# Gate and up projections of a SwiGLU block as one unit, with one of four k groups by Strassen's seven products

## The chip, the cores and the metric

The kernel runs on one core of a Trainium2 chip. The metric is device microseconds of one execution, the median of several runs: 2181.53 us before the change (three runs, 2178.58 to 2182.27). The profile shows one further execution of 2179.35 us; its span, from the first to the last instruction, is 2177.2 us. Engines are called as the profile calls them: PE (TensorE; PEld its weight loads), DVE (VectorE), ACT (ScalarE), POOL (GpSimd), SP (SyncE, which here only issues DMAs).

## The reference

One decoder layer on 256 tokens with 2048 channels, all in float32:

```python
def swiglu(x, w_gate, w_up, w_down):
    return (jax.nn.silu(x @ w_gate) * (x @ w_up)) @ w_down

h = h + 0.5 * swiglu(rms_norm(h, ffn1_norm[l]), ffn1_w_gate[l], ffn1_w_up[l], ffn1_w_down[l])
...
h = h + jnp.concatenate([ret, swa.astype(h.dtype)], axis=-1) @ w_out[l]
h = h + memory_cross_attention(rms_norm(h, xa_norm[l]), rms_norm(mem, mem_norm[l]),
                               xa_wq[l], xa_wkv[l], xa_wo[l])
h = h + 0.5 * swiglu(rms_norm(h, ffn2_norm[l]), ffn2_w_gate[l], ffn2_w_up[l], ffn2_w_down[l])
return rms_norm(h, final_norm)
```

Between the two feed-forward networks (FFN 1 and FFN 2) stand retention, sliding-window attention and cross-attention to a memory; the change doesn't touch them. w_gate and w_up are 2048 x 5632, w_down is 5632 x 2048.

## The kernel before

**Precision.** Float32 products are made of a high and a low half. `halves` (L71, L76) writes the high half on ACT (a copy that rounds to float32r) and the low half on DVE (value minus high half). `three` (L450 to L454) then makes three matmuls for each product: high by high, high by low, low by high. Weights are split right before use, a piece of 128 x 1024 at a time, into the tiles wh and wl (four buffers each); the normalized activations are split once into the tiles blk.

**Tiling.** The activations are the stationary operand (128 channels by 128 tokens), the weights the moving one (512 columns). A `Unit` computes 512 columns for all 256 tokens: its accumulator acc has two PSUM banks, one for each token half, and there are two such accumulators. A *step* takes one piece of weights, two k tiles of 128, and makes 2 token halves x 2 k tiles x 3 = 12 matmuls. The 2048 input channels are 16 k tiles, in four *k groups* of four (`norm.blocks`, tiles blk), so a gate or up unit has 8 steps. An FFN has 11 column blocks b of 512. For each, a gate unit and then an up unit run. `gate_done` applies silu with the row scale on ACT (L489), `up_done` multiplies on DVE (L496). `cross` then turns the block, so that its columns lie on partitions: two DVE transposes (L430) into a tile t4k, a DMA from SP into a DRAM tile box (L434), four DMAs from POOL back into t4k (L439), and `halves_of` splits the result into a blk tile `acts[b]` (an ACT copy and a DVE subtraction for each token half).

**Order.** `run_stream` (L230) walks over all steps of all units. It splits the weights of a step three steps ahead (`prepare`, LOOKAHEAD) and loads them eight steps ahead (`fetch`, AHEAD; three buffers wf of two pieces, one DMA of 1 MB from SP each). A clock counts steps; `later` queues work for a number of steps ahead: the box's write after 1, its read after 2, `halves_of` after 6 (TURN). Each engine runs its own instructions in one fixed order, set when the program is built: a scheduler may move an instruction past others of its engine, and then the order stands.

**Down projection.** In both FFNs column blocks 0 to 5 form a first group and 6 to 10 a second. After a group's gate and up units come four down units (one for each 512 output columns, nb), whose steps run over the group's blocks in order, two steps for each. In FFN 2, `turn_h` sends the residual through `cross` too, 19, 35, 51 and 67 steps after the last block of the residual is there.

## Time and profile before

| | |
|---|---|
| time, median of 3 runs (range) | 2181.53 us (2178.58 to 2182.27) |
| the profiled execution | 2179.35 us, span 2177.2 us |
| DVE, ACT, POOL busy | 1285.3, 1025.8, 149.5 us |
| HBM read, written | 443.08 MB, 33.55 MB |
| mean granted TensorE clock | 0.999 |

A row of the groups gives line, engine and operation, output and inputs by the program's names, shape and count; then busy time and the mean of one in ns; then the engine's idle time ahead of these instructions and what ended it. A row of the timeline gives start, duration, engine, line, operation, and in brackets the idle time before it and its releaser. A row of the windows gives the stretch and its length, then the busy time and count of PE, PEld, DVE, ACT and POOL, the granted clock, the DMA engines' share and GB/s. The records of matmuls overlap (389 ns each, one every 227 ns), so their pace is read from their starts.

### The profile page before, as it was taken

The numbers are of one execution on the slowest core, as the hardware profiler recorded it, in microseconds if no ns is written. First come the engines' busy times: TensorE is split into PE (matmuls) and PEld (weight loads), VectorE is DVE, ScalarE is ACT, GpSimd is POOL, SyncE is SP. The second block draws the span as 40 slices with busy tenths as digits, with TensorE's granted clock in tenths as the row PEclk, the third lists the DMA queues.
The fourth block names the chain that finished last, engine by engine and source line by source line (L and its number), as shares of the span: only waits on it lengthen the run. The fifth ranks groups of instructions, "written<-read, shape, count | busy, mean of one in ns | idle before, by whom it ended". The sixth has DMA issues, their size and how long they took to land.

```text
span 2177.2 us, 25112 instructions
## 1 busy us (share of the span) xinstructions
PE 2164.3 (99%) x9772; PEld 1793.3 (82%) x9772; DVE 1285.3 (59%) x1509; ACT 1025.8 (47%) x1260; POOL 149.5 (7%) x257
## 2 busy tenths in 40 slices
PE   9999999999999999999999999999999999999998
PEld 7888888888888888888888888888888888888886
DVE  6555555555556678787675655575555544555554
ACT  6444444444445554546454544454444433444443
POOL 0000000000001010100111100000101000000000
PEclk9999999999999999999999999999999999999999
DMA  7666677666667666556867765676767655666664
GB/s 271 232 221 213 213 232 222 222 213 221 224 216 252 216 216 222 193 186 238 265 231 244 225 216 174 204 243 216 247 222 256 216 193 193 213 213 213 225 210 145
DMA packets 137528, 478.27 MB, mean 220 GB/s; under 512 B 11713, under 2 KB 12481, under 8 KB 137281
## 3 DMA queue, kind: packets, MB, share of 16 engines
q1 hardware_dynamic: 125600, 445.03, 59.5%
q0 software_dynamic: 11520, 31.47, 6.2%
q8 instruction: 76, 1.25, 0.2%
q14 instruction: 44, 0.35, 0.0%
q10 hardware_dynamic: 288, 0.18, 0.0%
HBM read 443.08 MB, written 33.55 MB: 219 GB/s over the span
## 4 chain that ended last, share of the span: by engine, by line
PE 95%; DMA 2%; DVE 1%; issue 1%; ACT 0%; POOL 0%; SPq 0%; ACTq 0%; POOLq 0%; DVEq 0%
PE acc L452 31%; PE acc L453 31%; PE acc L454 31%; DMA wf<-in_ffn_w_up 1%; DMA t4k<-box 1%; DVE wl L76 1%; DMA box<-t4k 0%; PE tmp L454 0%; PE tmp L453 0%; PE tmp L452 0%; ACT wh L71 0%; PE tmp L656 0%; PE tmp L637 0%; PE tmp L603 0%; PE tmp L730 0%
## 5 line engine op out<-in xcount | busy, mean ns | idle before, releaser
L76 DVE TENSOR_TENSOR wl<-wf,wh 128x1024 fp32r<-128x1024 f32 (+1 forms) x776 | 941.4, 1217 | 782.8 <-ACT wh L71 779.0
L71 ACT ACTIVATE wh<-wf 128x1024 fp32r<-128x1024 f32 (+1 forms) x776 | 815.7, 1055 | 982.4 <-PE acc L454 940.2
L452 PE MATMUL acc<-wh,blk 128*128 128x512 f32 (+1 forms) x3104 | 1207.1, 389 | 1.7 <-ACT wh L71 1.1
L453 PE MATMUL acc<-wl,blk 128*128 128x512 f32 (+1 forms) x3104 | 1205.3, 388 | 0.8 <-DVE wl L76 0.8
L454 PE MATMUL acc<-wh,blk 128*128 128x512 f32 (+1 forms) x3104 | 1204.6, 388 | 0.0
L452 PEld LDWEIGHTS acc<-wh,blk 128*128 128x128 f32 x3104 | 582.9, 188 | 124.4 <-issue 2.3
L453 PEld LDWEIGHTS acc<-wl,blk 128*128 128x128 f32 x3104 | 583.0, 188 | 119.7 <-DVE wl L76 1.8
L454 PEld LDWEIGHTS acc<-wh,blk 128*128 128x128 f32 x3104 | 582.9, 188 | 119.9 <-DVE blk L340 0.2
L439 POOL DMA_DIRECT2D t4k<-box x240 | 139.0, 586 | 1760.5 <-DMA box<-t4k 1092.0
L71 ACT ACTIVATE blk<-t4k 128x512 fp32r<-128x512 f32 (+3 forms) x84 | 46.6, 601 | 51.5 <-DMA t4k<-box 51.3
L430 DVE STREAM_TRANSPOSE t4k<-t2k 128x512 f32<-128x512 f32 x88 | 57.6, 689 | 13.9 <-ACT t2k L71 13.8
L76 DVE TENSOR_TENSOR blk<-t4k,blk 128x512 fp32r<-128x512 f32 (+2 forms) x76 | 46.9, 657 | 27.0 <-ACT blk L71 26.5
L489 ACT ACTIVATE t2k<-acc,n 128x512 f32<-128x512 f32 x44 | 27.8, 684 | 26.9 <-PE acc L454 26.9
L496 DVE SCALAR_TENSOR_TENSOR t2k<-acc,n,t2k 128x512 f32<-128x512 f32 x44 | 31.0, 746 | 6.4 <-PE acc L454 6.4
L71 ACT ACTIVATE blk<-h,gains 128x256 fp32r<-128x256 f32 x64 | 27.3, 495 | 0.6 <-DVE h L463 0.6
L340 DVE SCALAR_TENSOR_TENSOR blk<-h,gains,blk 128x256 fp32r<-128x256 f32 x64 | 26.8, 477 | 0.0
L377 DVE TENSOR_TENSOR t2k<-t2k,t2k 128x512 f32<-128x512 f32 x35 | 24.1, 687 | 1.8 <-ACT t2k L373 0.3
L463 DVE TENSOR_TENSOR h<-h,t4k 128x512 f32<-128x512 f32 x32 | 20.6, 684 | 0.6 <-DMA t4k<-box 0.6
L373 ACT ACTIVATE t2k<-h 128x512 f32<-128x512 f32 x32 | 18.2, 617 | 2.1 <-DVE h L463 2.1
L626 ACT ACTIVATE t2k<-t2k,nmx 128x128 f32<-128x128 f32 (+1 forms) x32 | 14.2, 446 | 10.3 <-DVE nmx L623 8.3
L453 PE MATMUL tmp<-blk,blk 128*128 128x256 f32 x64 | 18.1, 283 | 0.0
L454 PE MATMUL tmp<-blk,blk 128*128 128x256 f32 x64 | 18.1, 283 | 0.0
(117 smaller groups left out, 417.1 us busy)
## 6 DMA issues: line engine op xcount, KB each, us to landing
wf<-in_ffn_w_down SPq DMA_DIRECT2D x88, 1024.0 KB, 5.0
wf<-in_ffn_w_gate SPq DMA_DIRECT2D x87, 1024.0 KB, 5.3
wf<-in_ffn_w_up SPq DMA_DIRECT2D x87, 1024.0 KB, 5.7
box<-t4k SPq DMA_DIRECT2D x60, 512.0 KB, 3.2
t4k<-box POOLq DMA_DIRECT2D x240, 128.0 KB, 5.5
wf<-in_w_in_rqk SPq DMA_DIRECT2D x16, 1024.0 KB, 6.5
wf<-in_w_in_rvg SPq DMA_DIRECT2D x16, 1024.0 KB, 5.4
wf<-in_w_out SPq DMA_DIRECT2D x16, 1024.0 KB, 5.3
```

Source lines behind the costliest of these rows:

```text
L71: return nc.scalar.activation(dst, src, AF.Copy, **kw)
L76: nc.vector.tensor_tensor(lo, src, hi, ALU.subtract)
L340: nc.vector.scalar_tensor_tensor(x[:, k, 1, :], v[:, k, :], g, x[:, k, 0, :], ALU.mult, ALU.subtract)
L377: nc.vector.tensor_tensor(self.sums, self.sums, y, ALU.add)
L430: nc.vector.transpose(z[:, t, :].rearrange("p (g q j) -> p q g j", g=4, q=4), squares_of(v))
L439: nc.gpsimd.dma_start(z[32 * g : 32 * g + 32].rearrange("p t (i n) -> p (t i) n", i=4), far[g])
L452: nc.tensor.matmul(o, ah, bh, start=start, stop=False)
L453: nc.tensor.matmul(o, ah, bl, start=False, stop=False)
L454: nc.tensor.matmul(o, al, bh, start=False, stop=stop)
L463: nc.vector.tensor_tensor(v, v, out[t], ALU.add)
L489: nc.scalar.activation(gated[b][t], acc[:, t, :], AF.Silu, scale=norm.scale(t))
L496: nc.vector.scalar_tensor_tensor(s[t], acc[:, t, :], norm.scale(t), s[t], ALU.mult, ALU.mult)
```

## The change

For every column block but the first of each FFN, gate and up become one unit, `Twin`. It has two accumulators, one for gate (f = 0) and one for up (f = 1). K groups 0, 1 and 2 run in 12 plain steps of 12 matmuls, called p0 to p11 here. K group 3 (SEVEN) is seen as a 2 x 2 block matrix product: token halves by pairs of k tiles, and pairs of k tiles by gate or up columns. Seven products of blocks, s0 to s6, take the place of the eight, in the Winograd form of Strassen's scheme, each with 6 matmuls (two k tiles, three halves). They stand behind p2 to p8, one each. Three of them accumulate straight into acc, four go into a PSUM tile tmp and are added by DVE. Four products need differences of weight blocks, which DVE makes in place (in `prepare`) before they are split. The sums of the activation blocks are made once per FFN (`sums_of`). The weights of k group 3 are loaded into two blk tiles instead of wf tiles. At the end of a Twin `parts` adds the accumulators to the sums; silu and the product with the gate then read SBUF. FFN 1 keeps its groups of six and five column blocks; FFN 2 has groups of four, four and three.

```diff
+SEVEN = 3
...
+    class Twin:
+
+        then, n, per_half = None, 512, False
+
+        def __init__(self, weights, index, norm, sums, done):
+            self.w = [w[2 * index : 2 * index + 2] for w in weights]
+            self.norm, self.lhs, self.sums, self.done = norm, norm.blocks, sums, done
+            self.acc, self.products, self.wide = [None, None], {}, []
+            units.append(self)
+
+        def steps(self):
+            plain = [(b, f, i) for b in range(4) if b != SEVEN for f in range(2) for i in range(2)]
+            out = []
+            for at, (b, f, i) in enumerate(plain):
+                out.append((self, b, range(2 * i, 2 * i + 2), f, at < 4 and i == 0, at + 4 - 2 * f >= len(plain) and i == 1 and b == plain[-1][0]))
+                if 2 <= at < 9:
+                    out.append((self, SEVEN, None, at - 2, False, False))
+            return out
+
+        def fetch(self, at, steps, loaded):
+            _, b, ks, f, first, _ = steps[at]
+            if ks is None:
+                return
+            pair = load_pair(self.w[f], b)
+            other = next(i for i in range(at + 1, len(steps)) if steps[i][2] is not None)
+            loaded[at], loaded[other] = pair
+            if first:
+                x = blk(F32).rearrange("p k c s -> p (k c s)").rearrange("p (f n) -> p f n", f=2)
+                nc.sync.dma_start(x, self.w[f][:, SEVEN].rearrange("f p n -> p f n"))
+                self.wide.append(x.rearrange("p f (k n) -> p k f n", n=S))
+
+        def prepare(self, kind):
+            (g0, g1), (u0, u1) = ([x[:, i::2] for i in range(2)] for x in self.wide)
+            src = (g0, g1, u1, g0, u0, u1, g1)[kind]
+            if kind > 2:
+                a, b = ((u0, g0), (u1, u0), (u1, g0), (g1, u1))[kind - 3]
+                nc.vector.tensor_tensor(src, a, b, ALU.subtract)
+            wh, wl = (wpool.tile([P, 1024], F32R, tag=x, name=nm(x)) for x in ("wh", "wl"))
+            halves(*(x.rearrange("p (k f n) -> p k f n", k=2, f=2) for x in (wh, wl)), src)
+            return [x.rearrange("p (k n) -> p k n", n=512) for x in (wh, wl)]
+
+        def multiply(self, kind, wh, wl):
+            x = self.lhs[SEVEN]
+            if kind in (0, 3, 4, 5):
+                o = self.products[kind] = tmp_ps()
+            else:
+                o = self.acc[kind == 2][:, int(kind == 6), :]
+            for j in range(2):
+                if kind in (0, 1, 6):
+                    k, t = 2 * j + (kind > 0), int(kind == 6)
+                    a = [x[:, k, c, t * P : (t + 1) * P] for c in range(2)]
+                else:
+                    i = {2: 3, 3: 0, 4: 2, 5: 1}[kind]
+                    a = [self.sums[0][:, c, i, j, :] for c in range(2)]
+                three(o, *a, wh[:, j, :], wl[:, j, :], kind in self.products and j == 0, kind in self.products and j == 1)
+            if kind == 0:
+                later(1.5, self.first_copy)
+            if kind == 5:
+                later(1, self.first_sums)
+                later(2, self.second_sums)
+
+        def add(self, out, a, b):
+            nc.vector.tensor_tensor(out, a, b, ALU.add)
+            return out
+
+        def first_copy(self):
+            self.u1 = t2k()
+            copy(self.u1, self.products[0])
+
+        def first_sums(self):
+            p = self.products
+            self.u2 = self.add(t2k(), self.u1, p[5])
+            self.u3 = self.add(t2k(), self.u2, p[4])
+
+        def second_sums(self):
+            p5 = self.products[3]
+            self.u5 = self.add(t2k(), self.u3, p5)
+            self.u4 = self.add(self.u2, self.u2, p5)
+
+        def parts(self, f):
+            acc = self.acc[f]
+            if f == 0:
+                return [self.add(self.u1, self.u1, acc[:, 0, :]), self.add(self.u3, self.u3, acc[:, 1, :])]
+            return [self.add(x, x, acc[:, t, :]) for t, x in enumerate((self.u4, self.u5))]
+
+    def sums_of(norm, dst):
+
+        y = blk(F32).rearrange("p k c s -> p (k c s)")
+        x, s = y[:, :1024].rearrange("p (j k s) -> p j k s", j=2, k=2), y[:, 1024:].rearrange("p (i j s) -> p i j s", i=4, j=2)
+
+        def scale():
+            for k in range(4):
+                g = norm.gcol + 4 * SEVEN + k
+                copy(x[:, k // 2, k % 2, :], hT[SEVEN][:, k, :], scale=gains[:, g : g + 1])
+
+        def add():
+            (a11, a21), (a12, a22) = ([x[:, :, k, t * P : (t + 1) * P] for t in range(2)] for k in range(2))
+            for o, a, b, op in (
+                (0, a21, a22, ALU.add), (1, s[:, 0], a11, ALU.subtract), (2, a11, a21, ALU.subtract),
+                (3, a12, s[:, 1], ALU.subtract),
+            ):
+                nc.vector.tensor_tensor(s[:, o], a, b, op)
+
+        def part():
+            z = blk().rearrange("p k c s -> p (k c s)").rearrange("p (c i j s) -> p c i j s", c=2, i=4, j=2)
+            halves(z[:, 0], z[:, 1], s)
+            dst.append(z)
+        for i, fn in enumerate((scale, add, part)):
+            later(1 + i, fn)
...
+            if ks is None:
+                run_until(lambda: u.sums)
+                u.multiply(which, *ready.pop(at))
+                clock[0] += 0.5
+                continue
+            if isinstance(u, Twin):
+                if first:
+                    u.acc[which] = ps_acc.tile([P, 2, 512], F32, tag="acc", name=nm("acc"))
+                wh, wl = ready.pop(at)
+                for t in range(2):
+                    by_tokens(u, u.acc[which], x, wh, wl, ks, t, first, last)
+                clock[0] += 1
+                if last:
+                    u.done(which, u.parts(which))
+                continue
...
-    def ffn(norm, w_gate, w_up, down):
+    def ffn(norm, w_gate, w_up, down, groups):
...
+                sums_of(norm, sums)
+            return done
+
+        def both_done(b):
+            def done(f, x):
+                if f == 0:
+                    gated[b] = x
+                    for t in range(2):
+                        nc.scalar.activation(x[t], x[t], AF.Silu, scale=norm.scale(t))
+                    return
+                s = gated.pop(b)
+                for t in range(2):
+                    nc.vector.scalar_tensor_tensor(s[t], x[t], norm.scale(t), s[t], ALU.mult, ALU.mult)
+                turn(b, s)
             return done
 
         def up_done(b):
@@ -494,17 +641,24 @@
                 s = gated.pop(b)
                 for t in range(2):
                     nc.vector.scalar_tensor_tensor(s[t], acc[:, t, :], norm.scale(t), s[t], ALU.mult, ALU.mult)
-
-                def made(out):
-                    acts[b] = halves_of(out, blk())
-                cross(s, made)
+                turn(b, s)
             return done
 
-        for g, fbs in enumerate((range(0, 6), range(6, 11))):
+        def turn(b, s):
+
+            def made(out):
+                acts[b] = halves_of(out, blk())
+            cross(s, made)
+
+        sums = []
+        for g, fbs in enumerate(groups):
             for b in fbs:
+                if b > 0:
+                    Twin((w_gate, w_up), b, norm, sums, both_done(b))
+                    continue
                 Unit(w_gate, b, 512, norm.blocks, gate_done(b), range(4), pair=True)
                 Unit(w_up, b, 512, norm.blocks, up_done(b), range(4), pair=True)
-                if b == 0 and norm is not n1:
+                if norm is not n1:
                     together()
             down(g, acts, fbs)
 
@@ -538,7 +692,7 @@
         else:
             to_h(a["ffn1_w_down"], acts, 0.5, fbs, nmix, near_mix)
 
-    ffn(n1, a["ffn1_w_gate"], a["ffn1_w_up"], ffn1_down)
+    ffn(n1, a["ffn1_w_gate"], a["ffn1_w_up"], ffn1_down, (range(0, 6), range(6, 11)))
 
 
 
@@ -950,7 +1104,7 @@
 
     def ffn2_down(g, acts, fbs):
         for nb in range(4):
-            if g == 0:
+            if g < 2:
                 Unit(a["ffn2_w_down"], nb, 512, acts, lambda acc, nb=nb: first_down(nb, acc), fbs)
             elif nb < 3:
                 Unit(a["ffn2_w_down"], nb, 512, acts, lambda acc, nb=nb: last_down(nb, acc), fbs)
@@ -1000,7 +1154,7 @@
             for b in range(4):
                 later(19 + 16 * b, lambda b=b: turn_h(b))
 
-    ffn(n2, a["ffn2_w_gate"], a["ffn2_w_up"], ffn2_down)
+    ffn(n2, a["ffn2_w_gate"], a["ffn2_w_up"], ffn2_down, (range(0, 4), range(4, 8), range(8, 11)))
```

On VectorE, at the end of the gate and up projections of a block in the middle of FFN 1, before the change (t2k holds the gated block, wl are low halves of weights):

```order
L496 SCALAR_TENSOR_TENSOR t2k_1233<-acc_1241,n_103,t2k_1233 128x512
L496 SCALAR_TENSOR_TENSOR t2k_1234<-acc_1241,n_103,t2k_1234 128x512
L430 STREAM_TRANSPOSE t4k_1376<-t2k_1233 128x4x4x32
L430 STREAM_TRANSPOSE t4k_1376<-t2k_1234 128x4x4x32
L76 TENSOR_TENSOR wl_1381<-wf_1292,wh_1380 128x1024
L76 TENSOR_TENSOR wl_1399<-wf_1326,wh_1398 128x1024
```

The product with the gate reads the accumulator, and the splits of the next gate unit follow right behind the transposes.

The same place on VectorE after the change, at the end of a Twin; wl_1151 and wl_1189 belong to the products s0 and s1 of the next Twin, wl_1169 and wl_1206 to its steps p3 and p4:

```order
L238 TENSOR_TENSOR t2k_1071<-t2k_1071,acc_873 128x512
L238 TENSOR_TENSOR t2k_1085<-t2k_1085,acc_873 128x512
L635 SCALAR_TENSOR_TENSOR t2k_915<-t2k_1071,n_103,t2k_915 128x512
L635 SCALAR_TENSOR_TENSOR t2k_1073<-t2k_1085,n_103,t2k_1073 128x512
L563 STREAM_TRANSPOSE t4k_1146<-t2k_915 128x4x4x32
L563 STREAM_TRANSPOSE t4k_1146<-t2k_1073 128x4x4x32
L77 TENSOR_TENSOR wl_1151<-blk_1026,wh_1150 128x1024
L77 TENSOR_TENSOR wl_1169<-wf_1055,wh_1168 128x1024
L212 TENSOR_TENSOR blk_1026<-blk_1057,blk_1026 128x2x2x256
L77 TENSOR_TENSOR wl_1189<-blk_1026,wh_1188 128x1024
L212 TENSOR_TENSOR blk_1057<-blk_1057 128x2x2x256
L77 TENSOR_TENSOR wl_1206<-wf_1128,wh_1205 128x1024
```

Two sums stand ahead of the product with the gate, and the subtractions of weight blocks (L212) stand well ahead of the splits that need them.

On TensorE, the first down unit of FFN 2's last group, where it comes to the last block's activations (blk_15161), before the change:

```order
L453 MATMUL acc_15057<-wl_15128,blk_14867 128x512
L454 MATMUL acc_15057<-wh_15127,blk_14867 128x512
L452 MATMUL acc_15057<-wh_15143,blk_15161 128x512
L453 MATMUL acc_15057<-wl_15144,blk_15161 128x512
L454 MATMUL acc_15057<-wh_15143,blk_15161 128x512
```

The last block's matmuls follow those of the block before it.

The same place on TensorE after the change: acc_15865 is the first down unit, acc_15988 the second, blk_15939 the last block's activations:

```order
L586 MATMUL acc_15988<-wl_15936,blk_15338 128x512
L587 MATMUL acc_15988<-wh_15935,blk_15338 128x512
L585 MATMUL acc_15865<-wh_15879,blk_15939 128x512
L586 MATMUL acc_15865<-wl_15880,blk_15939 128x512
L585 MATMUL acc_15988<-wh_15956,blk_15657 128x512
L587 MATMUL acc_15865<-wh_15879,blk_15939 128x512
```

Before, the first down unit runs through. Now two steps of the second (24 matmuls with the group's first block) stand between the first unit's second block and its last, and one more matmul of the second unit stands inside that step.

More of the change, by code (lines that the diff above doesn't have):

```diff
@@ L232, in run_stream @@
         steps[:FIRST] = [x for y in zip(steps[: FIRST // 2], steps[FIRST // 2 : FIRST]) for x in y]
-        loaded = []
+        loaded, ahead = {}, [FIRST]
         for i in range(0, FIRST, 4):
@@ L249, in run_stream @@
                 both = [load_pair(steps[i + j][0].w, steps[i + j][3]) for j in range(2)]
-            loaded.extend(both[j][h] for h in range(2) for j in range(2))
+            loaded.update((i + 2 * h + j, both[j][h]) for h in range(2) for j in range(2))
         ready = {}
@@ L254, in fetch @@
         def fetch(upto):
-            while len(loaded) < min(upto, len(steps)):
-                at = len(loaded)
+            while ahead[0] < min(upto, len(steps)):
+                at = ahead[0]
+                ahead[0] += 1
+                if at in loaded:
+                    continue
                 u, piece = steps[at][0], steps[at][3]
-                if u.pair:
-                    loaded.extend(load_pair(u.w, piece))
+                if isinstance(u, Twin):
+                    u.fetch(at, steps, loaded)
+                elif u.pair:
+                    loaded.update(enumerate(load_pair(u.w, piece), at))
                 else:
                     two = at + 1 < len(steps) and steps[at + 1][0] is u and steps[at + 1][3] == piece + 1
-                    loaded.extend(load(u.w, piece, 1 + two))
+                    loaded.update(enumerate(load(u.w, piece, 1 + two), at))
         def prepare(upto):
@@ L268, in prepare @@
                 at = nxt[0]
-                if at == 0:
+                if steps[at][2] is None:
+                    ready[at] = steps[at][0].prepare(steps[at][3])
+                elif at == 0:
                     ready[at] = split(loaded[at], steps[at][0].n, 2, lambda k: n1.some(0, [hT[0][:, k : k + 1, :]], k))
@@ L284, in run_stream @@
         held = []
-        for at, (u, b, ks, _, first, last) in enumerate(steps):
+        for at, (u, b, ks, which, first, last) in enumerate(steps):
             if at < FIRST:
@@ L297, in run_stream @@
             x = u.lhs[b]
+            if ks is None:
[3 more added lines that the diff above has]
+                continue
+            if isinstance(u, Twin):
+                if first:
[7 more added lines that the diff above has]
+                continue
             if first:
@@ L496, in done @@
                     nc.vector.scalar_tensor_tensor(s[t], acc[:, t, :], norm.scale(t), s[t], ALU.mult, ALU.mult)
-                def made(out):
-                    acts[b] = halves_of(out, blk())
-                cross(s, made)
-            return done
-        for g, fbs in enumerate((range(0, 6), range(6, 11))):
+                turn(b, s)
+            return done
+        def turn(b, s):
[4 more added lines that the diff above has]
+        for g, fbs in enumerate(groups):
             for b in fbs:
+                if b > 0:
+                    Twin((w_gate, w_up), b, norm, sums, both_done(b))
+                    continue
                 Unit(w_gate, b, 512, norm.blocks, gate_done(b), range(4), pair=True)
                 Unit(w_up, b, 512, norm.blocks, up_done(b), range(4), pair=True)
-                if b == 0 and norm is not n1:
+                if norm is not n1:
                     together()
```

## Prediction

> **What bounds the kernel now.** First the page's busy times and its chain, then the list of what TensorE waits for.
>
> ```profile
> PE 2164.3 (99%) x9772; PEld 1793.3 (82%) x9772; DVE 1285.3 (59%) x1509; ACT 1025.8 (47%) x1260; POOL 149.5 (7%) x257
> PE 95%; DMA 2%; DVE 1%; issue 1%; ACT 0%; POOL 0%; SPq 0%; ACTq 0%; POOLq 0%; DVEq 0%
> PE tmp L93 <- POOL ident masks.py:199: 1.4, 1, 1.4
> PE acc L452 <- ACT wh L71: 1.1, 1, 1.1
> ```
>
> TensorE is the bound: 2164 of 2177 us busy, 95% of the chain, and no wait of it is longer than 1.4 us. So a matmul that goes is worth its full pitch, unless something now hidden comes late. Busy TensorE need not be TensorE at its pace, so the pace is checked on a stretch of FFN 2, between the ends of two gate-up pairs (VectorE's timeline, and the same stretch by engine):
>
> ```profile
> 1929.25 1.41 DVE L496 SCALAR_TENSOR_TENSOR t2k<-acc,n,t2k 128x512 f32<-128x512 f32 x2 [0.40 <-PE acc L454]
> 1972.77 1.41 DVE L496 SCALAR_TENSOR_TENSOR t2k<-acc,n,t2k 128x512 f32<-128x512 f32 x2 [0.40 <-PE acc L454]
> 1929.00:1972.60 43.60, 43.60 (x194) 36.08 (x194) 23.31 (x22) 19.29 (x20) 2.31 (x4) 1.00 0.65 218
> ```
>
> A pair has 16 steps of 12 matmuls, 192 in all, and comes every 1972.77 - 1929.25 = 43.52 us: 0.2267 us a matmul, **2.72 us a step**, at clock 1.00, with VectorE busy 23.31, ScalarE 19.29 and the DMA engines 65%.
>
> **What goes.** In each of the 20 Twins the four steps of k group 3 (48 matmuls) become seven products of 6 (42). 20 x 6 = 120 matmuls go, as TensorE's order also counts (9593 rows before, 9473 now): 120 x 0.2267 = **27.2 us**. A product lasts 1.36 us, a Twin 12 x 2.72 + 7 x 1.36 = 42.16 us, 1.36 less than a pair. The products have the same shapes, so I price them at the same pitch.
>
> **What is added beside TensorE.** Prices come from the groups by shape:
>
> ```profile
> L76 DVE TENSOR_TENSOR wl<-wf,wh 128x1024 fp32r<-128x1024 f32 x768 | 936.1, 1222 | 775.9 <-ACT wh L71 772.1
> L71 ACT ACTIVATE wh<-wf 128x1024 fp32r<-128x1024 f32 x768 | 811.0, 1060 | 978.2 <-PE acc L454 940.2 <-DMA wf<-in_ffn_w_up 7.6 <-issue 6.2
> L962 DVE SCALAR_TENSOR_TENSOR blk<-acc,blk 128x512 f32<-128x512 f32 x14 | 9.0, 686 | 2.8 <-PE acc L454 2.8
> ```
>
> A Twin splits 19 pieces instead of 16 (3 more on both engines), subtracts weight blocks four times (128x1024, no row; two SBUF inputs as in the split, so 1.22) and adds eight times from PSUM (128x512, as L962, 0.69). VectorE: 23.31 + 7 x 1.22 + 8 x 0.69 = 37.4 us of 42.16, 89%. ScalarE: 19.29 + 3 x 1.06 + one copy of 0.6 = 23.1. VectorE has room on average; the question is the start of a Twin, where the sums pile up. Let T be the first matmul of the next Twin. Timeline of the end of a pair:
>
> ```profile
> 1711.45 0.39 PE L452 MATMUL acc<-wh,blk 128*128 128x512 f32 x1
> 1711.65 1.41 DVE L496 SCALAR_TENSOR_TENSOR t2k<-acc,n,t2k 128x512 f32<-128x512 f32 x2 [0.40 <-PE acc L454]
> 1712.97 1.29 DVE L430 STREAM_TRANSPOSE t4k<-t2k 128x512 f32<-128x512 f32 x2
> 1714.19 2.50 DVE L76 TENSOR_TENSOR wl<-wf,wh 128x1024 fp32r<-128x1024 f32 x2
> 660.98 1.23 DVE L76 TENSOR_TENSOR wl<-wf,wh 128x1024 fp32r<-128x1024 f32 x1 [1.50 <-ACT wh L71]
> 662.12 1.29 DVE L463 TENSOR_TENSOR h<-h,t4k 128x512 f32<-128x512 f32 x2
> ```
>
> VectorE starts 0.20 after T. Back to back, instructions overlap: two of L496 advance it 1.32, two transposes 1.22, a split 1.14 (660.98 to 662.12). In a Twin it runs from T+0.20: two last sums 1.32, two products with the gate 1.32, two transposes 1.22, so T+4.06; then, in the order shown above, s0, p3, a subtraction, s1, a subtraction, p4, s2 and two subtractions, 9 x 1.14, so p5 starts at T+14.3 and is ready at 15.6. TensorE takes p5 after five plain steps and three products, 5 x 2.72 + 3 x 1.36 = 17.7: **2.1 us of cover**. Buffers do not bind earlier: p5 uses the one that p3 frees at T+12.2, s3 the one of s1 at T+13.6.
>
> Behind s3 both engines have the halves of the last block's activations, which wait for the box in DRAM. That round trip, from L496 to ScalarE's first copy, is read where the copy waited for the DMA (starts of L496 at 227.41, 1583.12, 1711.65 and 2059.81):
>
> ```profile
> 227.41 1.41 DVE L496 SCALAR_TENSOR_TENSOR t2k<-acc,n,t2k 128x512 f32<-128x512 f32 x2 [0.40 <-PE acc L454]
> 243.91 1.15 ACT L71 ACTIVATE blk<-t4k 128x512 fp32r<-128x512 f32 x2 [1.84 <-DMA t4k<-box]
> 1583.12 1.40 DVE L496 SCALAR_TENSOR_TENSOR t2k<-acc,n,t2k 128x512 f32<-128x512 f32 x2
> 1602.04 1.15 ACT L71 ACTIVATE blk<-t4k 128x512 fp32r<-128x512 f32 x2 [7.15 <-DMA t4k<-box]
> 1728.73 1.15 ACT L71 ACTIVATE blk<-t4k 128x512 fp32r<-128x512 f32 x2 [2.42 <-DMA t4k<-box]
> 1729.79 2.00 ACT L71 ACTIVATE wh<-wf 128x1024 fp32r<-128x1024 f32 x2
> 2059.81 1.41 DVE L496 SCALAR_TENSOR_TENSOR t2k<-acc,n,t2k 128x512 f32<-128x512 f32 x2 [0.40 <-PE acc L454]
> 2074.92 1.15 ACT L71 ACTIVATE blk<-t4k 128x512 fp32r<-128x512 f32 x2 [0.45 <-DMA t4k<-box]
> ```
>
> 16.5, 18.9, 17.1 and 15.1 us. The longest falls where `turn_h` uses the same path in FFN 2. Two sums now stand ahead of L496, so the data land at T + 0.20 + 1.32 + trip. Behind them p6 needs the two copies (1.06, from 1728.73 to 1729.79), its ScalarE half (1.06) and its VectorE half (1.23): 3.35. TensorE takes p6 at 17.7 + 2.72 + 1.36 = T+21.8, its low half 0.23 later. So a trip up to 22.0 - 3.35 - 1.52 = **17.1 us costs nothing**; each us more stalls TensorE one us. FFN 1 stays below. In FFN 2 the two Twins beside `turn_h` (its copies also stand in ScalarE's row) pay 0 to 1.8 each; I take 1.5 for both together, between the rows.
>
> **The seams.** The down projection needs the last block's activations after the others. With six or five blocks that was 12 or 10 steps away, and the trip was hidden. FFN 2 now has groups of four, four and three. With four, block 3 is due after 6 steps, T+16.3. With three it would be 4 steps, T+10.9, but TensorE's order has two steps of the next column block pulled ahead (shown above), so again T+16.3. It can go on at landing + 0.9 (copy 0.62 and subtraction 0.69, less two matmuls, since only the third reads the low half). Stall: 1.52 + trip + 0.9 - 16.3, which is 1.2 at 15.1 and 3.2 at 17.1. The 15.1 was measured at the last group itself, so 1.2 there; for the others I take the middle, 2.2 each: **5.6 us**, between 3.6 and 9.6. FFN 1 keeps its groups. The third group also adds eight additions of 0.69 on VectorE, beside splits that wait for ScalarE (L76, 776 us idle): nothing.
>
> **The rest.** Building the sums of the normalized blocks (six ScalarE and five VectorE instructions, once per FFN) falls in the first Twin; in FFN 1 L496 came 2 us after T there (55.05), and p6 is then 0.4 us late: 0.5, bounds 0 and 2. The loads are the same bytes; group 3's two megabytes go to tiles of their own, asked for eight steps before the next Twin (p7 to p11 with two products, 16.3 us), where a megabyte lands in about 5:
>
> ```profile
> wf<-in_ffn_w_gate SPq DMA_DIRECT2D x87, 1024.0 KB, 5.3
> ```
>
> The four PSUM tiles of the products are freed by the sums before the next Twin's s0, and the accumulators by the last sums before p0 and p2 write them: nothing, and a wait of at most one sum, 0.69, per Twin if not.
>
> **The sum.** 27.2 - 5.6 - 1.5 - 0.5 = **19.6 us**. The profiled execution took 2179.35 (span 2177.2), so 2159.7; it lies 2.2 below the median 2181.5, on which I forecast **2162** (0.9% faster). Its own range: at best 27.2 - 3.6, so 2158; at worst 27.2 - 9.6 - 3.6 - 2, so 2169.5.
>
> [...] The box is read by DMAs issued on POOL:
>
> ```profile
> L439 POOL DMA_DIRECT2D t4k<-box x240: 582/584/745, 61.6 to 2067.7; - x120
> ```
>
> 240 issues took 582 to 745 ns, median 584, with VectorE busy 59%. [...] If four issues all took 745, a trip would be 0.64 longer, the seams 1.9 us more: 2164.
>
> **Rivals.**
> - *VectorE becomes the bound.* From T to p6 it has 12 large and 8 small instructions. At 1.38 us a large one instead of 1.14, p6 is late; at 1.45 by 0.8 us in each of 20 Twins, 16 us, and the time is 2178, no change. For it: 89% busy, subtractions in place, sums that read PSUM while TensorE writes it. Against: the measured advance of 1.14 and L962's 0.69 with PSUM as source.
> - *The box trip becomes the bound, and the kernel slower.* 17 trips end inside a Twin, 3 at FFN 2's seams. At 18.9, the longest row, each Twin pays 1.8 (30.6) and each seam 5.0 (15): 27.2 - 45.6 - 0.5 = -18.9, so 2200. It decides from a mean trip of 18.0 us, where 17 x 0.9 + 3 x 4.1 uses up the gain. For it: box writes queue on SP among the loads. Against: 15 to 16.5 wherever `turn_h` is silent, and the order leaves SP one load right behind the box, as before.
> - *The issues slow down* as above: 2164.
> - *Small stalls that I don't see* (an accumulator, a load in the first Twins), some 0.4 us a Twin: 8 us less, 2170.
>
> **How the numbers follow.** Chances: forecast 0.66, VectorE 0.10, trip 0.12, issues 0.04, small stalls 0.08. About 0.2% (4.4 us) is what a measurement can tell from no change. Faster: 0.66 + 0.04 + 0.08 = 0.78; same: 0.10; slower: 0.12. The range runs from the forecast's best, 2157 with a spare us, over small stalls to the edge of the VectorE rival, 2177.
>
> **What would show it.** 9652 matmuls; products at 0.227 us pitch; a Twin every 42.2 us; TensorE idle before the activations' first matmuls at FFN 2's three seams, some us each, and almost nowhere else. Idle before p5 or p6 with VectorE as releaser is the first rival, behind ScalarE's copies of t4k the second. The forecast is wrong if Twins come at 42.9 us or more.

## The result and the profile after

The change took the median from 2181.9 us (4 runs, 2178.58 to 2183.34) to **2165.84 us** (4 runs, 2163.22 to 2168.41): a ratio of 0.9931, 95% interval 0.9919 to 0.9942. The forecast was 2162. The profiled execution has a span of 2161.2 us, 16.0 less than before; the sum had said 19.6. A later repeat of the same kernel (experiment 7) gave 2159.22, and the eight runs together have their median at 2162.2. So the time came out, but the profile shows that the terms did not.

First what was right. The page's busy row and TensorE's three longest groups of waits (engine, operand, line, releaser; us in total, times, longest), then VectorE's timeline at the end of two Twins, and the stretch between them by engine:

```profile
PE 2142.7 (99%) x9652; PEld 1773.1 (82%) x9652; DVE 1548.7 (72%) x1827; ACT 1106.0 (51%) x1350; POOL 149.1 (7%) x257
PE acc L585 <- ACT blk L72: 4.0, 3, 3.0
PE acc L586 <- DVE wl L77: 2.5, 3, 1.6
PE acc L585 <- ACT wh L72: 1.5, 2, 1.0
```

```profile
184.62 1.41 DVE L635 SCALAR_TENSOR_TENSOR t2k<-t2k,n,t2k 128x512 f32<-128x512 f32 x2
226.78 1.41 DVE L635 SCALAR_TENSOR_TENSOR t2k<-t2k,n,t2k 128x512 f32<-128x512 f32 x2
```

```profile
184.62:226.78 42.16, 42.16 (x188) 34.92 (x187) 35.96 (x38) 22.93 (x24) 2.30 (x4) 1.00 0.64 224
```

A Twin lasts 42.16 us to the hundredth, TensorE never stops in it, and VectorE is busy 35.96 us (37.4 was estimated). The 27.2 us are there. These waits, 8.0 us together (1.2 of them in the first 11 us of the span), say where some of them went; the chain of the page doesn't, so the trace is cut into four parts at rows that both kernels have: the first matmul behind the sums of squares of a normalization (L388 before, L521 now). Those rows on TensorE's timeline, before and after:

```profile
47.27 0.48 PE L452 MATMUL acc<-wh,blk 128*128 128x512 f32 x1
753.38 0.37 PE L453 MATMUL acc<-wl,blk 128*128 128x256 f32 x1
1476.77 0.48 PE L453 MATMUL acc<-wl,blk 128*128 128x512 f32 x1
```

```profile
46.60 0.49 PE L585 MATMUL acc<-wh,blk 128*128 128x512 f32 x1
743.40 0.36 PE L586 MATMUL acc<-wl,blk 128*128 128x256 f32 x1
1468.27 0.48 PE L586 MATMUL acc<-wl,blk 128*128 128x512 f32 x1
```

The differences of these starts, and of the last one to the span's end, for this and three later kernels (us; in brackets what is saved against before; ten Twins in each FFN, so 60 x 0.2267 = 13.6 is due in each):

| | start | FFN 1 | between | FFN 2 and end | span |
|---|---|---|---|---|---|
| before | 47.27 | 706.11 | 723.39 | 700.4 | 2177.2 |
| the change | 46.60 | 696.80 (9.3) | 724.87 (-1.5) | 692.9 (7.5) | 2161.2 |
| 1: tables later | 48.53 | 692.49 (13.6) | 724.72 (-1.3) | 692.8 (7.6) | 2158.5 |
| 3: blocks alternate | 47.68 | 698.52 (7.6) | 726.19 (-2.8) | 688.0 (12.4) | 2160.4 |
| 4: both | 46.67 | 692.50 (13.6) | 726.29 (-2.9) | 686.4 (14.0) | 2151.9 |

**FFN 1 gives back 4.3 us, all but 0.1 in its first Twin.** SP's timeline there, after (first fence) and before (second); then the product with the gate and the copy on ScalarE that ends the box's round trip, and the same copy before; TensorE's timeline; and two stretches with the granted clock:

```profile
57.03 0.37 SPq L567 DMA_DIRECT2D box<-t4k  x1
57.50 1.45 SPq L312 DMA_DIRECT2D wf<-in_ffn_w_up  x1
60.28 0.37 SPq L312 DMA_DIRECT2D wf<-in_ffn_w_gate  x1
60.70 0.46 SPq L678 DMA_DIRECT2D ctab<-in_ctab  x1
```

```profile
57.69 0.37 SPq L434 DMA_DIRECT2D box<-t4k  x1
58.80 14.83 SPq L201 DMA_DIRECT2D wf<-in_ffn_w_up  x4
73.67 0.46 SPq L524 DMA_DIRECT2D ctab<-in_ctab  x1
```

```profile
54.39 0.75 DVE L643 SCALAR_TENSOR_TENSOR t2k<-acc,n,t2k 128x512 f32<-128x512 f32 x1
72.72 1.15 ACT L72 ACTIVATE blk<-t4k 128x512 fp32r<-128x512 f32 x2 [5.35 <-DMA t4k<-box]
```

```profile
69.87 1.15 ACT L71 ACTIVATE blk<-t4k 128x512 fp32r<-128x512 f32 x2 [1.88 <-DMA t4k<-box]
```

```profile
74.87 0.50 PE L585 MATMUL acc<-wh,blk 128*128 128x512 f32 x1 [0.49 <-ACT wh L72]
77.00 0.50 PE L586 MATMUL acc<-wl,blk 128*128 128x512 f32 x1 [1.63 <-DVE wl L77]
...
78.03 0.63 PE L587 MATMUL acc<-wh,blk 128*128 128x512 f32 x1
78.46 0.63 PE L585 MATMUL acc<-wh,blk 128*128 128x512 f32 x1
```

```profile
78.40:81.70 3.30, 3.30 (x10) 2.54 (x9) 3.09 (x3) 0.44 (x1) 0.00 (x0) 0.54 0.10 15
81.70:86.00 4.30, 4.30 (x21) 3.55 (x20) 2.45 (x2) 2.18 (x3) 0.00 (x0) 1.00 0.93 362
```

The box's round trip, from the product with the gate (54.39) to the copy (72.72), took 18.3 us; before it took 14.8 (55.05 to 69.87). The rotary table ctab, 512 KB, was issued at 73.67 before, behind four weight loads that wait for buffers. Now it is issued at 60.70, just ahead of the box's reads (from 61.16). The copy comes late, behind it the splits for the next step, and TensorE waits 2.12 us. Then something follows that no wait shows: the clock falls to half, and eight matmuls come every 0.43 us instead of 0.227, 1.6 us more. TensorE counts as busy all the while. The gaps beyond the pitch (2.56) and the 1.6 make 4.2. That the trip sets the wait shows across the eleven profiles with Twins (the change and the experiments): in this Twin TensorE's waits are the trip less 15.9 to 16.2 us (16.6 gave 0.69, 17.5 gave 1.52, 19.0 gave 2.77), and none where the trip took 14.3 or 14.9.

**FFN 2 gives back 6.1 us, most of it at its last seam.** The copy, TensorE's timeline and the clock there:

```profile
2100.73 1.15 ACT L72 ACTIVATE blk<-t4k 128x512 fp32r<-128x512 f32 x2 [3.94 <-DMA t4k<-box]
```

```profile
2098.03 0.39 PE L587 MATMUL acc<-wh,blk 128*128 128x512 f32 x1
2101.41 0.50 PE L585 MATMUL acc<-wh,blk 128*128 128x512 f32 x1 [3.00 <-ACT blk L72]
...
2102.30 0.64 PE L587 MATMUL acc<-wh,blk 128*128 128x512 f32 x1
2102.74 0.63 PE L585 MATMUL acc<-wh,blk 128*128 128x512 f32 x1
```

```profile
2102.30:2105.50 3.20, 3.20 (x9) 2.52 (x9) 1.61 (x2) 0.53 (x1) 0.00 (x0) 0.50 0.17 24
2105.50:2110.00 4.50, 4.50 (x21) 3.68 (x21) 2.18 (x3) 2.02 (x2) 0.00 (x0) 1.00 0.55 224
```

The trip (L635 at 2083.34) took 17.4 us, the stall is 3.00, and again the clock halves, for some 1.6 us more. The other two seams cost waits of 0.58 and 0.39 (trips of 15.0 and 14.8), and the clock stays. Here too the wait follows the trip: at 21 of the 22 seams of FFN 2 that waited in the profiles with Twins it is the trip less 14.3 to 14.45 us. Why the last trip is the longest isn't settled; the loads issued behind the box are of the same kind as at the second seam.

### The profile page after: what moved, and what is told of

It is laid out like the page before. It is cut to its first block, busy times and chain, and to the rows that moved or that the text cites. A ratio compares the mean times of both kernels' runs of the same rounds, so it can differ in the third digit from the quotient of the medians.

```text
span 2161.2 us, 25375 instructions
## 1 busy us (share of the span) xinstructions
PE 2142.7 (99%) x9652; PEld 1773.1 (82%) x9652; DVE 1548.7 (72%) x1827; ACT 1106.0 (51%) x1350; POOL 149.1 (7%) x257
## 4 chain that ended last, share of the span: by engine, by line
PE 92%; DMA 3%; DVE 2%; issue 1%; ACT 1%; POOL 0%; SPq 0%; ACTq 0%; POOLq 0%; DVEq 0%
PE acc L585 28%; PE acc L586 28%; PE acc L587 28%; DMA t4k<-box 2%; PE tmp L585 2%; PE tmp L586 2%; PE tmp L587 2%; DVE wl L77 1%; DMA wf<-in_w_in_rqk 0%; DMA box<-t4k 0%; POOL t4k L572 0%; DMA wf<-in_ffn_w_up 0%; PE tmp L810 0%; ACT blk L72 0%; PE tmp L791 0%
## 5 line engine op out<-in xcount | busy, mean ns | idle before, releaser
L77 DVE TENSOR_TENSOR wl<-wf,wh 128x1024 fp32r<-128x1024 f32 (+1 forms) x696 | 844.5, 1217 | 484.8 <-ACT wh L72 479.4
L72 ACT ACTIVATE wh<-wf 128x1024 fp32r<-128x1024 f32 (+1 forms) x696 | 732.0, 1055 | 809.7 <-PE acc L587 761.5
L585 PE MATMUL acc<-wh,blk 128*128 128x512 f32 (+1 forms) x2904 | 1131.3, 390 | 5.4 <-ACT blk L72 4.0
L586 PE MATMUL acc<-wl,blk 128*128 128x512 f32 (+1 forms) x2904 | 1128.8, 389 | 2.5 <-DVE wl L77 2.5
L587 PE MATMUL acc<-wh,blk 128*128 128x512 f32 (+1 forms) x2904 | 1128.2, 389 | 0.0
L585 PEld LDWEIGHTS acc<-wh,blk 128*128 128x128 f32 x2904 | 546.2, 188 | 121.8 <-ACT blk L72 5.4
L587 PEld LDWEIGHTS acc<-wh,blk 128*128 128x128 f32 x2904 | 546.1, 188 | 112.7 <-DVE blk L77 0.6
L72 ACT ACTIVATE wh<-blk 128x1024 fp32r<-128x1024 f32 x140 | 148.3, 1060 | 78.4 <-PE acc L587 60.6
L77 DVE TENSOR_TENSOR wl<-blk,wh 128x1024 fp32r<-128x1024 f32 x140 | 170.6, 1218 | 8.7 <-ACT wh L72 3.2
L212 DVE TENSOR_TENSOR blk<-blk,blk 128x1024 f32<-128x1024 f32 x60 | 73.4, 1224 | 1.4
L563 DVE STREAM_TRANSPOSE t4k<-t2k 128x512 f32<-128x512 f32 x88 | 57.7, 691 | 13.9 <-ACT t2k L72 13.8
L585 PE MATMUL tmp<-wh,blk 128*128 128x512 f32 x160 | 62.4, 390 | 0.0
L587 PE MATMUL tmp<-wh,blk 128*128 128x512 f32 x160 | 62.2, 389 | 0.0
L586 PE MATMUL tmp<-wl,blk 128*128 128x512 f32 x160 | 62.2, 389 | 0.0
```

What stands on the lines that cost most here:

```text
L72: return nc.scalar.activation(dst, src, AF.Copy, **kw)
L77: nc.vector.tensor_tensor(lo, src, hi, ALU.subtract)
L212: nc.vector.tensor_tensor(src, a, b, ALU.subtract)
L563: nc.vector.transpose(z[:, t, :].rearrange("p (g q j) -> p q g j", g=4, q=4), squares_of(v))
L585: nc.tensor.matmul(o, ah, bh, start=start, stop=False)
L586: nc.tensor.matmul(o, ah, bl, start=False, stop=False)
```

## The experiments

The theory: the Strassen saving is whole, and what is missing is given back at two places, where a late box trip stalls TensorE and the stall halves the clock. Rivals: VectorE sets the pace, the slow stretches have causes of their own, or the smaller groups cost by themselves. In all diffs the lines are those of the changed kernel, in experiment 5 of the kernel before. By their medians alone experiments 1 and 3 (ratios 0.9905 and 0.9901) don't differ from the repeat of the unchanged kernel (0.9903, experiment 7); what an edit does is read from the parts of its trace.

### 1. The tables' loads later

```diff
-    later(24, load_tables)
+    later(100, load_tables)
```

> The loads of the rotary tables and sinks, which stand right behind the box's write and two weight loads in SP's queue in the first Twin of FFN 1, are asked for 76 steps later; nothing else changes. Theory (a late box trip, then a halved clock): the trip of that Twin falls from 18.3 us to under 16, TensorE's waits of 0.49 and 1.63 us go, the granted clock stays at 1.00 between 78.4 and 81.7 us, and the span falls by about 5 us to 2156 (ratio to the kernel before about 0.991). Rival (the sums of the blocks on VectorE and ScalarE make the first Twin late, whatever the loads): the waits on VectorE's wl stay, the span stays within 1 us of 2161.

Measured: median 2160.06 us, ratio 0.9905 (0.9892 to 0.9919), span 2158.5. In the first Twin the trip is 14.3 us, TensorE doesn't wait, the clock stays, and FFN 1 saves its 13.6 us to the tenth (table above), while the other parts are as in the changed kernel. The span is 2.5 us above the expected one, mostly because this execution began 1.9 us later (48.53 against 46.60). That looks like proof, but experiment 7 qualifies it.

### 2. Eleven, then 24 idle matmuls at the last seam

```diff
+            if b == 10 and u.lhs is not n2.blocks and at == len(steps) - 20:
+                last_pe = look()[mybir.EngineType.PE]
+                fill = tmp_ps()
+                for _ in range(11):
+                    ins = nc.tensor.matmul(fill[:, :P], ident, ident, start=True, stop=True)
...
+                        order(last_pe, ins)
```

The second kernel has 24 in place of 11.

> At the last seam, ahead of the first step on block 10, TensorE gets 11 matmuls of 128x128 on the identity whose result nobody reads (about 2.3 us). The data come no earlier. Theory (the idle time of 3.0 us is what halves the clock afterwards): the wait shrinks to under 1 us but the products and steps behind it start when they did; the clock stays at 1.00, the pitch at 0.227 us where it was 0.427, and the span is about 3 us shorter, 2158. Rival (the slow matmuls behind the seam wait for something else, weights or an operand): the pitch stays at 0.427 there and the span at 2161 or up to 2.3 longer.

> As the kernel with 11 matmuls on the identity ahead of the last seam, with 24 of them (about 5.2 us), which outlast the wait. With 11, 2.4 us of waiting were left and the clock halved all the same. Theory (idle time alone halves it): no wait at the seam over 0.5 us, the clock 1.00 and the pitch 0.227 us behind it. Rival (something else at this seam slows the matmuls behind it): half the clock, or a pitch of 0.43 us, at the same products again.

Measured: 2167.51 us, ratio 0.994 (0.9926 to 0.9954), and 2166.11, ratio 0.9933 (0.9915 to 0.9951). With 11 a wait of 2.43 us was left and the clock halved. TensorE's timeline with 24, and the stretch behind the seam:

```profile
2092.80 5.52 PE L420 MATMUL tmp<-ident 128*128 128x128 f32 x48
2100.12 0.50 PE L593 MATMUL acc<-wh,blk 128*128 128x512 f32 x1 [1.80 <-ACT blk L72]
```

```profile
2100.10:2104.00 3.90, 3.88 (x17) 3.12 (x18) 1.29 (x2) 1.05 (x2) 0.00 (x0) 1.00 0.18 69
```

As an intervention both missed: TensorE ran the idle matmuls in place of steps that it had taken ahead (one step with 11, both with 24), so they filled no idle time (with 24, 5.5 us for 5.4). What the second one shows is narrower: the trip happened to take 16.1 us, the wait was 1.80, and the same matmuls behind the same seam ran at clock 1.00. So they have no slowness of their own: at this seam the clock fell behind waits of 3.00 and 2.43 us, and not behind one of 1.80.

### 3. and 4. Two down units of FFN 2 alternate; and both edits

```diff
         for nb in range(4):
...
+            if nb == 1:
+                together()
```

> In FFN 2 the first two column blocks of the down projection of every group alternate step by step, as a gate-up pair does, so that the last block of the group is due two to four steps (5.4 to 10.9 us) later; the count of matmuls and the loads' bytes stay. Theory (the seams cost a stall each for the box trip, the last one a halved clock too): no TensorE wait over 0.3 us before the activations' first matmuls of FFN 2, clock 1.00 behind the last seam, 0.6 + 0.4 + 3.0 + 3.0 = 7 us gone, span 2154. Rival (groups of four, four and three cost by their loads or by the third group's additions, not by the wait): under 2 us gone, span 2159 or more.

> The later tables and the alternating blocks of the down projection together. Theory (two places, independent of each other, give back the whole difference): the two gains add, 5 + 7 = 12 us, span 2149, ratio to the kernel before 0.987. Rival (one cause behind both, such as the loads as a whole, so that what goes at one place comes back later): no more than the larger of the two, span 2154 or more.

Measured: 2160.18 us, ratio 0.9901 (0.9887 to 0.9915), span 2160.4; and for both edits 2157.62 us, ratio 0.9891 (0.9877 to 0.9905), span 2151.9. No row of waits names the activations' first matmuls any more. The whole list of TensorE's waits for both edits:

```profile
PE tmp L521 <- DVE t2k L518: 1.7, 1, 1.7
PE tmp L94 <- POOL ident masks.py:199: 1.4, 1, 1.4
PE tmp L765 <- DVE blk L77: 0.4, 1, 0.4
PE acc L586 <- DVE wl L77: 0.2, 1, 0.2
PE acc L585 <- ACT wh L72: 0.2, 1, 0.2
```

In the table FFN 1 saves 13.6 and FFN 2 14.0 us, 27.6 where 27.2 were due. In this execution the gains add, as the theory said, though the span is 2.9 us above the expected 2149: 1.4 us more go in the part between (the wait of 1.7 in the list, at FFN 2's normalization), and the half clock at the last seam was worth 1.6 us, not the 3.0 that I had expected. With alternating blocks alone FFN 2 saves 12.4; there a wait of 1.64 us at the same normalization halves the clock for eight matmuls of FFN 2, which is the missing 1.6. That execution also lost its FFN 1 gain in the first Twin (waits of 1.14 and 1.63, half the clock behind them), so the span missed the expected 2154 by 6.4. All of these spans vary by what happens at the places that an edit leaves alone.

### 5. The small groups without Strassen

```diff
-        for g, fbs in enumerate((range(0, 6), range(6, 11))):
+        for g, fbs in enumerate(groups):
...
+    ffn(n2, a["ffn2_w_gate"], a["ffn2_w_up"], ffn2_down, (range(0, 4), range(4, 8), range(8, 11)))
```

> The kernel before, with nothing of Strassen's scheme, but with the down projection of FFN 2 in groups of four, four and three. Theory (the groups cost their seams): waits of 0.5 to 3 us at one to three seams, and about 3 us more where a wait of over 2 us halves the clock behind it; in all 1 to 7 us slower than before, span 2178 to 2184. Rival (the seams are late only because Strassen's sums stand ahead of the last product with the gate): no wait there over 0.3 us, span within 1 us of 2177.

Measured: 2181.81 us (11 runs, 2180.14 to 2190.62) against 2180.49, ratio 1.0005 (0.9996 to 1.0015). The medians differ by 1.3 us, which the interval doesn't tell from nothing. The profiled execution is the slowest of the eleven, and shows what a seam can cost; a copy for `turn_h` on ScalarE, TensorE's timeline and the clock behind it:

```profile
1626.66 1.15 ACT L71 ACTIVATE blk<-t4k 128x512 f32<-128x512 f32 x2 [5.26 <-DMA t4k<-box]
```

```profile
1648.45 0.80 PE L452 MATMUL acc<-wh,blk 128*128 128x512 f32 x1 [6.39 <-ACT blk L71]
```

```profile
1648.40:1653.80 5.40, 5.35 (x13) 4.15 (x14) 2.52 (x3) 1.47 (x2) 0.00 (x0) 0.50 0.30 80
```

Two things meet at this seam. `turn_h`'s copy waits for its box, the splits behind it in ScalarE's order come late, and VectorE starts the last block's product with the gate only at 1629.94, some 4 us after TensorE had done its part (TensorE stops at 1642.06, six steps or 16.3 us behind that point); then the block's own trip takes 17.8 us. So the groups cost next to nothing in most executions, and some 10 us in this one. The rival that only Strassen's sums make the seams late falls: the last seam, with a trip of 15.2 us and nothing late ahead of it, waits 0.48 us too.

### 6. More work on VectorE in every Twin

Four, eight or sixteen subtractions that nobody reads:

```diff
                 turn(b, s)
+                extra = t2k()
+                for _ in range(8):
+                    nc.vector.tensor_tensor(extra, s[1], s[0], ALU.subtract)
```

> The changed kernel, and at the end of each of the 20 Twins four more subtractions of 128x512 on VectorE behind the transposes, whose result nobody reads (about 2.5 us each time). Theory (VectorE has about 2 us of cover at the start of a Twin): TensorE waits 0 to 0.6 us in each Twin, too little for the clock, so 0 to 12 us on top of 2166. Rival (VectorE already sets the pace of a Twin): all 2.5 us show, 20 times, 2216.

> As the kernel with four subtractions, with eight of them (about 5.1 us). Theory: 3 us of it are beyond the cover, in each of 20 Twins, 60 us; and if a wait of that length halves the clock for about 3.2 us behind it, as at the two places of the changed kernel, up to 3 us more each time: 2226 without the clock, 2260 to 2290 with it, and rows at half clock behind most of the waits. Rival (the two slow stretches had a cause of their own at their places): waits of 3 us with a clock of 1.00 behind them, 2226.

> Sixteen of the extra subtractions at each Twin's end instead of eight. With eight VectorE was busy 39.92 of 42.16 us in a Twin, with none 35.96, so 0.5 us each. Theory (VectorE becomes the bound when its own time exceeds the Twin): 43.9 us of VectorE, Twins 43.9 us apart or more, 20 x 1.7 = 35 us and above on top of 2166, so 2200; TensorE waits for wl in every Twin, and where a wait is about 2 us the clock halves behind it. Rival (what binds is the start of a Twin, not VectorE's whole time): the 4 us that eight more take there come on top in every Twin, 80 us, 2246.

Measured: 2163.76 us, ratio 0.9924 (0.9911 to 0.9938), with four; 2168.21, ratio 0.9942 (0.9924 to 0.996), with eight; 2212.81, ratio 1.0145 (1.0125 to 1.0165), with sixteen. One Twin with eight, and a pair of Twins with sixteen, by engine:

```profile
184.62:226.78 42.16, 42.16 (x188) 34.91 (x187) 39.92 (x46) 22.50 (x25) 2.31 (x4) 1.00 0.61 224
```

```profile
120.00:211.00 91.00, 87.13 (x374) 69.32 (x373) 89.06 (x107) 44.78 (x49) 4.62 (x8) 1.00 0.59 208
```

With four and with eight the Twin is still 42.16 us, and the expected 2226 with eight was wrong by 58. But the experiment did not use up the cover of 2 us at the start of a Twin. The eight are spread over its first 13 us, one ahead of each split, and the scheduler put the subtractions of weight blocks behind them: ahead of p5's split stand four in the changed kernel, two with four extra operations and one with eight. In the changed kernel p5's low half is ready 15.7 us after T, the first matmul of the Twin (15.6 in the prediction, needed at 17.7), with eight extra operations at 16.2. So the cover was as reckoned, and the error was to take VectorE's order as given. With sixteen VectorE is busy 89.06 of 91.00 us, and a Twin lasts 45.5: now VectorE is the bound. It needs 44.5 a Twin rather than 43.9, since the extra operations cost about 0.54 each and not 0.5. So VectorE, in the order that the scheduler chooses, did not bind with 39.92 us of work in a Twin of 42.16 and did with 44.5: what makes it the bound is between eight and sixteen more operations away. What a late start of a Twin costs in a fixed order was not tested.

### 7. The changed kernel and both edits again, on one chip

> The changed kernel once more, on the chip and in the rounds of the next two. Theory: waits at the first Twin of FFN 1 and at the last seam again, median 2164 to 2168, ratio to the kernel before 0.993. Rival (the two places were an accident of one profiled execution): neither wait over 1 us, span under 2156.

> Later tables and alternating blocks of the down projection once more, beside the changed kernel. Theory: no wait in the first Twin or at a seam of FFN 2, 6 to 12 us below the changed kernel in the same rounds, median 2155 to 2159. Rival: under 4 us below it.

Measured: 2159.22 us (2156.81 to 2161.22), ratio 0.9903 (0.9886 to 0.9919), for the changed kernel; 2153.76 us (2151.66 to 2161.68), ratio 0.9881 (0.986 to 0.9902), for both edits, 5.5 us less (6 to 12 were expected). With the first measurements each has eight runs, with medians of 2162.2 and 2155.7. The intervals measured side by side overlap; the difference rests on both measurements showing it, and on the parts of the trace.

The waits of the changed kernel at these places in this execution (span 2154.9):

```profile
PE acc L585 <- ACT blk L72: 2.4, 2, 1.7
PE acc L586 <- DVE wl L77: 1.6, 3, 1.0
PE acc L585 <- ACT wh L72: 0.5, 1, 0.5
```

They are the same places with shorter trips (first Twin 16.9, last seam 16.1), no wait over 1.7 us, and the clock stays at 1.00: 6.3 us less with the same program. The expectation of 2164 to 2168 was wrong in just that. And with the tables later (the profiled execution of both edits is the slowest of its four, 2161.68), the first Twin's trip was 18.4 us this time, against the expectation of no wait there; TensorE's timeline, and the clock behind it:

```profile
77.08 0.50 PE L586 MATMUL acc<-wl,blk 128*128 128x512 f32 x1 [1.63 <-DVE wl L77]
```

```profile
77.00:82.00 5.00, 4.92 (x22) 4.09 (x23) 5.00 (x6) 2.51 (x3) 0.00 (x0) 1.00 0.08 16
```

FFN 1 saves 10.9 us in this execution, and FFN 2 10.8: no seam waits, but a wait of 2.88 us at FFN 2's normalization halves the clock behind it, 2.7 us more. So the tables are not the whole cause. Eight profiles that load them there have trips of 16.6 to 19.0 us, the three that load them later 14.3, 14.9 and 18.4. In the last of these the box's four reads took 9.8 us to land (6.4 in the first execution with both edits) behind the same weight loads; why is open.

## Why the prediction was right, and where not

The forecast of 2162 lay 3.8 us below the first median and on the median of all eight runs, in its range either way. That it falls on the latter is luck: one and the same program had spans of 2161.2 and 2154.9 us, and the sum of 19.6 was 3.6 above what the first of them shows. By its steps:

- **What goes.** "120 x 0.2267 = 27.2 us": right. 9652 matmuls, a Twin of 42.16 us as forecast, and 27.6 us saved in the two FFNs when nothing is given back (experiment 4).
- **The first Twin.** "FFN 1 stays below" and "0.5, bounds 0 and 2": mis-sized, 4.3 in the profile shown. The step that failed is that the trip there stays short enough: it took 18.3 us, and 16.6 to 19.0 in the eight profiles that load the tables there. The reason given, "the loads are the same bytes", overlooks SP's order: the tables' load, which stood behind four weight loads, now stands ahead of the box's reads. That this order is the cause is shown in part: without it the trip was 14.3 and 14.9 us in two profiles, but 18.4 in a third, so what else lengthens it stays open. The half microsecond had been priced for the building of the activations' sums, and the runs show no wait for them: where the trip was short, the first Twin didn't wait.
- **FFN 2's seams.** The mechanism was right, and its formula is so but for a constant half microsecond: 1.52 + trip + 0.9 - 16.3, the trip less 13.9, gives 3.5, 1.1 and 0.9 us for the trips measured (17.4, 15.0 and 14.8), against waits of 3.00, 0.58 and 0.39, the trip less 14.4. The trips were mis-sized: "the 15.1 was measured at the last group itself", but that was a single execution; in the profiles with Twins the last trip was 15.0 to 17.4, in most of them over 16. The term of 5.6 was measured as 6.1, near by luck, with its parts the wrong way round (last seam 1.2 forecast, about 4.7 measured; the others 4.4 and 1.3).
- **The Twins beside `turn_h`.** 1.5 forecast, nothing measured: no TensorE wait over 0.2 us in the profile shown between FFN 2's start and its first seam.
- **The clock** was left out: stalls were priced at their length. At two places the half clock added some 1.6 us each.
- **VectorE as the bound** did not happen, and experiment 6 shows it far off as long as the scheduler may reorder its work. **The issues** did not slow down: with VectorE busy 72% instead of 59% their median is 582 ns, 2 ns lower:

```profile
L572 POOL DMA_DIRECT2D t4k<-box x240: 582/582/745, 61.2 to 2091.3; - x120
```

In both kernels the 745 ns belong to the first issue alone, and the other 239 took 627 at most; with sixteen more subtractions in every Twin the median is 584. That all four issues of a trip take 745 was an estimate, which these traces don't show.
- **The box trip as the bound**: trips of 14.8 to 15.7 us in the Twins of FFN 2 behind the first ones, so it stayed far from the mean of 18.0 that would have used up the gain. But it is what took back nearly all that was taken back: the rival's mechanism was real in the first Twin of FFN 1 and at the seams.

So the FFNs gave back 10.4 us where 7.6 were forecast. The rest of the way from 19.6 to 16.0 is the part between them, 1.5 us longer without a changed step, less 0.7 us at the start. All of the 1.5 falls at two places where TensorE waits for low halves from VectorE: waits of 0.35 us at 777.79 and 0.61 at 807.94, which by the starts of the same matmuls in both kernels cost 0.6 and 0.9. Why these halves come later than before isn't settled.

## What to carry to other kernels

When instructions go from the bound engine, walk every DMA queue in its new order, also loads that belong to a later part of the program: one that moved ahead here was not in the changed code. Price a stall of a busy TensorE not at its length alone but with the half clock that may follow it (1.6 us more behind waits of 2.12 and 3.00 here), which shows in the granted clock and in the pitch, not in the waits. And cut two traces at rows that both have and compare the parts: the spans moved by 6 us from run to run, while a part in which nothing waited came out within 0.4 us of what was due. Before adding work to an engine as a test, look where the scheduler puts the rest of its work.

## What the runs showed of the hardware

Two stalls of TensorE in the changed kernel were followed by half its clock, one of 2.12 us (clock 0.54 from 78.40 to 81.70) and one of 3.00 (0.50 from 2102.30 to 2105.50). In the traces of the change and the experiments, behind the first 15 us, and counting waits that end less than 2.5 us apart together: of waits of 2.4 us or more all 8 were followed by half the clock, of 2.05 to 2.21 us 6 out of 9, of 1.5 to 2.03 us 1 out of 8, and of shorter ones none. The length alone doesn't decide: at FFN 2's normalization a wait of 1.64 us was followed by half the clock in experiment 3, and one of 1.69 was not with both edits. Two waits of the kernel with sixteen subtractions, at the same place of two Twins, and the clock behind each:

```profile
255.79 0.50 PE L586 MATMUL acc<-wl,blk 128*128 128x512 f32 x1 [2.07 <-DVE wl L77]
...
610.30 0.50 PE L586 MATMUL acc<-wl,blk 128*128 128x512 f32 x1 [2.08 <-DVE wl L77]
```

```profile
256.70:260.20 3.50, 3.50 (x11) 2.69 (x10) 3.50 (x5) 0.00 (x0) 0.00 (x0) 0.53 0.00 0
610.20:614.20 4.00, 3.90 (x17) 3.24 (x18) 4.00 (x6) 0.00 (x0) 0.00 (x0) 1.00 0.00 0
```

The clock of the changed kernel falls three times behind the first 15 us, the last time with TensorE's work over:

```profile
77.00:78.00 1.00, 1.00 (x4) 0.86 (x5) 1.00 (x2) 0.66 (x1) 0.00 (x0) 1.00 0.00 0
78.00:81.41 3.41, 3.41 (x9) 2.65 (x8) 3.41 (x4) 0.15 (x1) 0.00 (x0) 0.50 0.01 1
2101.50:2102.10 0.60, 0.60 (x3) 0.40 (x3) 0.60 (x2) 0.60 (x2) 0.00 (x0) 1.00 0.08 31
2102.11:2105.51 3.40, 3.40 (x10) 2.69 (x9) 1.80 (x2) 0.72 (x1) 0.00 (x0) 0.50 0.16 25
2155.70:2156.71 1.01, 0.00 (x0) 0.00 (x0) 0.34 (x1) 0.53 (x1) 0.00 (x0) 1.00 0.46 172
2156.72:2161.20 4.48, 0.00 (x0) 0.00 (x0) 0.00 (x0) 0.00 (x0) 0.00 (x0) 0.50 0.54 197
```

The first two stretches last 3.41 us each, and from fall to fall it is 2024.10 and 54.61 us, 593 and 16 times 3.4133. Steps of that length, counted from the fall at about 256.9 in the kernel with sixteen subtractions, give an estimate for its two waits: the one that ends at 255.79 lies whole in one step, and of the one that ends at 610.30 only 1.8 us do. That would tell these two apart, but the wait of 1.64 us in experiment 3 is shorter still, so what decides isn't settled. The slow stretch mostly lasted 3 to 3.5 us and cost about 1.6; behind four of the five waits of 2.77 us and above it lasted 5 to 6.2 and cost 2.4 to 3.0.
